# One layer with attention, retention and a squared-ReLU MLP: the sums of the first MLP product on one engine only, and one staging buffer at another address

## Chip, cores and metric

The kernel runs on one core of a Trainium2 chip. Its time is the device time of one execution in microseconds (us). A core has five engines that work at once, each through its own queue in program order: TensorE (PE in the profile; its weight loads are PEld), VectorE (DVE), ScalarE (ACT), GpSimd (POOL) and SyncE (SP), which here only issues the transfers between HBM and the on-chip memory.

## What is computed

The last stage of the layer is this MLP, in float32, on 2048 tokens of 1024 features:

```python
h = x * (1.0 + sc2) + sh2
f = jnp.square(jax.nn.relu(h @ w_ff1[l])) @ w_ff2[l]
x = layer_norm(ALPHA * x + gt2 * f, ln2_g[l], ln2_b[l])
```

w_ff1 is 1024 x 4096, w_ff2 is 4096 x 1024. Ahead of it stand the input norm, the conditioning, two mixers (latent attention and retention) and their output product; the change doesn't touch them.

## The kernel before, in words

**Precision.** Each float32 operand of a matmul is split in two: ScalarE rounds it to a high part (line 128), and an engine subtracts that to give a low part (line 131). A product is then three matmuls, high by high, low by high and high by low (lines 136 to 138, `mm3`).

**The first MLP product** (`split_h` and `up`) uses a Strassen-like scheme with seven block products P1 to P7 in place of eight. The tokens are taken in two halves; in each half sixteen steps c each make 256 of the 4096 columns, and the loop takes them in pairs (c, c+1) through the seven products in turn, so a pair is 14 products of 12 matmuls 128x512 each: P1, P1, P5, P5, P6, P6, P7, P7, P2, P2, P3, P3, P4, P4, on the accumulators u_X, u_Z, u_Y, u_W, and again u_X, u_Z, u_W. For each c four blocks of w1 (`w`, 128x512) are loaded into two buffers per block position; four of the seven products need a sum or a difference of blocks first, made in place (line 1077 in `prod`), before ScalarE and VectorE split the result into `w1h` and `w1l`. The ring of `w1h` and `w1l` holds five products (W1B).

**The choice of engine.** Line 1077 runs on VectorE where half is 0 and c is below 4 (W1V), and on GpSimd everywhere else: 16 times and 112 times. `split_h` makes the activation operands (`hh`, `hl`) of the seven products once per half, each in two pieces of 128x1024: a difference of blocks (line 1060) where the product needs one, and the split. For half 0 both pieces are on VectorE; for half 1, done during the last pair of half 0, the first piece is VectorE's and the second GpSimd's.

**Behind the products** VectorE adds accumulators (lines 1104 to 1122: `u`, `v`), ScalarE applies relu and square (lines 1093, 1094) and SyncE stores 256 KB to `g_d` (line 1095). `u` has two buffers, `v` three, and `r`, which takes the accumulator u_X directly, one. Spread over the same loop, a generator prepares w2 for the second product (`w2r`, `w2s`, lines 1132 to 1141) on VectorE and ScalarE.

**The second MLP product** (`down`) starts when the first ends. It loads `a` from `g_d` (line 1266) and its weights `wP` from `wt_d` (line 1276), splits `a` into `gP1h`, `gP1l` and so on, and accumulates in d_W, d_Z, d_X. Its pools lie where the pools of the first product lay, so a load into them waits until the earlier tile at that address is read or stored.

**What sets the order.** A scheduler with a timeline model of its own orders each engine's instructions when the kernel is built; each engine then works strictly in that order. The pools of the first product are stacked in the order of the tuple HSO: numbers are the operand pools of the seven products (index 0 to 6), "u" the pool of `u` and `v`, "w" that of `w1h` and `w1l`, "s" that of `w2s`, and "o" that of `r` (2 KB of each partition).

Of the kernel before, what the change touches and what calls it, by code (L numbers as in the profile page):

```python
# [14 lines left out]
OP = mybir.AluOpType  # L15
# [33 lines left out]
NLA = 3  # L49
HSS = "VVVVVVV"  # L50
HSL = "VVVVVVV"
HSO = 6, 5, "u", 4, 3, 2, "s", "o", 1, "w", 0
SRT = 29
LB = 18
HFB = 4
# [11 lines left out]
W1V = 4  # L67
# [50 lines left out]
def build(nc, tc, I, out, upto=9, dbg=None):  # L118
    dbg = {} if dbg is None else dbg
    V, A, G, T, Q = nc.vector, nc.scalar, nc.gpsimd, nc.tensor, nc.sync  # L120
# [3 lines left out]
    def split(x, hi, lo, hi_eng=None, lo_eng=None, log=None):  # L124
        hi_eng = hi_eng or A
        lo_eng = lo_eng or V
        if hi_eng is A:
            A.activation(hi, x, AF.Copy)  # L128
        else:
            hi_eng.tensor_copy(hi, x)  # L130
        i = lo_eng.tensor_tensor(lo, x, hi.bitcast(F32), op=OP.subtract)  # L131
        if log is not None:
            log.append(i.ins)

    def mm3(ps, sh, sl, mh, ml, start, stop, more=False):
        T.matmul(ps, sh, mh, start=start, stop=False, skip_group_check=more)  # L136
        T.matmul(ps, sh, ml, start=False, stop=False, skip_group_check=more)  # L137
        T.matmul(ps, sl, mh, start=False, stop=stop, skip_group_check=more)  # L138
# [805 lines left out]
    for n in range(2):  # L944
        p = (wo0, wo1)[n]
        wo.append([[p.tile([P, 512], R32, name=f"wo_{x}{n}_{k}") for x in "hl"] for k in range(KD)])
        for i in range(4):
            st = WOS[n][i]
            ks = range(2 * i, 2 * i + 2)
# [82 lines left out]
    hs4 = [None] * 7  # L1032
    for i in HSO:
        if i == "w":
# [10 lines left out]
    def split_h(half, o):  # L1045
        raw = {}
        for j, n in ((0, 0), (0, 1), (1, 1), (1, 0)):
            raw[j, n] = t = hraw.tile([P, 4, 512], F32, tag="raw", name=f"h4_{half}_{j}{n}")
            Q.dma_start(t, h2_d[border[2 * half + n]].rearrange("k p c -> p k c")[:, 4 * j:4 * j + 4, :])
        b11, b12, b22, b21 = raw[0, 0], raw[0, 1], raw[1, 1], raw[1, 0]  # L1050
        for x, (name, src, sub) in enumerate((("P1", b11, None), ("P5", b12, (b12, b11)), ("P6", b12, (b22, b12)),
                                              ("P7", b11, (b12, b11)), ("P2", b21, None), ("P3", b22, None),
                                              ("P4", b12, (b21, b12)))):
            p = hs4[x]
            hh = p.tile([P, 4, 512], R32, tag="hh", name=f"hh{half}_{name}")
            hl = p.tile([P, 4, 512], R32, tag="hl", name=f"hl{half}_{name}")
            for q in range(2):
                ks = slice(2 * q, 2 * q + 2)
                if sub:
                    (V, G if half else EN[HSS[x]])[q].tensor_tensor(src[:, ks], sub[0][:, ks], sub[1][:, ks], op=OP.subtract)  # L1060
                split(src[:, ks], hh[:, ks], hl[:, ks], A, (V, G if half else EN[HSL[x]])[q])
            o[name] = hh, hl
            yield

    def up(half, c, H):
        raw = []
        for m, j in ((0, 0), (1, 0), (1, 1), (0, 1)):
            t = w1r.tile([P, 512], F32, tag=f"r{m}{j}", name=f"w1_{half}_{c}_{m}{j}")
            with tc.issue_after(wodma) if half == 0 and c < 2 else nullcontext():
                Q.dma_start(t, I["w_ff1"][2 * c + m][:, 4 * j:4 * j + 4].rearrange("p k c -> p (k c)"))  # L1070
            raw.append(t)
        a11, a21, a22, a12 = raw
        ps = {}

        def prod(name, src, op, ch, start, sub=None):
            if sub:
                (V if half == 0 and c < W1V else G).tensor_tensor(src, *sub, op=op)  # L1077
            wh = w1p.tile([P, 512], R32, tag="wh", name=f"w1h{half}_{c}_{name}")
            wl = w1p.tile([P, 512], R32, tag="wl", name=f"w1l{half}_{c}_{name}")
            split(src, wh, wl, A, V, lows)  # L1080
            if start:
                ps[ch] = psf[c % 2].tile([P, 512], F32, tag="f", name=f"u{half}_{c}_{ch}")
            hh, hl = H[name]
            for k in range(4):
                ks = slice(k * P, (k + 1) * P)
                mm3(ps[ch], wh[:, ks], wl[:, ks], hh[:, k], hl[:, k], start and k == 0, k == 3, not start)

        def o(name, tag="o"):
            return (o4 if tag == "o" else o4b).tile([P, 512], F32, tag=tag, name=f"{name}{half}_{c}", bufs=dict(o=OO, u=2, v=OV)[tag])

        def act(x, m, n):
            r = o("r") if x is ps["X"] else x
            A.activation(r, x, AF.Relu)
            A.activation(r, r, AF.Square)
            Q.dma_start(g_d[2 * c + m][:, (2 * half + n) * 512:(2 * half + n + 1) * 512], r)

        prod("P1", a11, None, "X", True)
        yield
        prod("P5", a21, OP.add, "Z", True, (a21, a22))
        u = o("u", "u")  # L1100
        A.activation(u, ps["X"], AF.Copy)
        yield
        prod("P6", a21, OP.subtract, "Y", True, (a21, a11))
        V.tensor_tensor(u, u, ps["Y"], op=OP.add)
        yield
        prod("P7", a11, OP.subtract, "W", True, (a22, a21))
        v = o("v", "v")
        V.tensor_tensor(v, u, ps["Z"], op=OP.add)
        yield
        prod("P2", a12, None, "X", False)  # L1110
        V.tensor_tensor(v, v, ps["W"], op=OP.add)
        act(v, 1, 1)
        yield
        prod("P3", a21, OP.subtract, "Z", False, (a12, a21))
        act(ps["X"], 0, 0)
        yield
        prod("P4", a22, None, "W", False)
        v = o("v", "v")
        V.tensor_tensor(v, u, ps["Z"], op=OP.add)
        act(v, 0, 1)  # L1120
        v = o("v", "v")
        V.tensor_tensor(v, u, ps["W"], op=OP.add)
        act(v, 1, 0)
# [24 lines left out]
    NCH = DFF // 256  # L1148
    H = {}
    first = split_h(0, H)  # L1150
    for half in range(2):
        todo = work(range(8 * half, 8 * half + 8))
# [3 lines left out]
        count = 0  # L1156
        Hn = {}
        nxt = split_h(1, Hn) if half == 0 else None
        for c in range(0, NCH, 2):
            pair = [up(half, x, H) for x in (c, c + 1)]  # L1160
# [236 lines left out]
```

## Time and profile before

| what | us |
|---|---|
| median of three runs (2575.91 to 2579.59) | 2579.45 |
| the profiled execution, its own time | 2581.13 |
| its span, first to last instruction | 2579.4 |
| TensorE busy in the span | 2435.3 |
| VectorE busy | 1791.5 |
| ScalarE busy | 1218.5 |
| GpSimd busy | 1134.5 |

The first MLP product lies between 1276 and 1938 us of the span: its first matmul starts at 1276.2, half 1 begins at about 1626, and the last matmul starts at 1937.6. The second product follows to the end. In the timeline views a row gives start, duration, engine, line, operation, written and read tile, a count where equal neighbours are merged, and in brackets the idle time before it with what ended that. Durations of neighbours on an engine overlap a little, so the pace of a queue is read from start to start.

### The profile page before, as it was taken

The page shows a single profiled execution, that of the slowest core. Times are in us where ns is not written, and L with a number is a line of the kernel's source. Part 1 is how long each engine was busy: PE and PEld are TensorE (multiplying, and loading weights), DVE is VectorE, ACT ScalarE, POOL GpSimd, SP SyncE. Part 2 cuts the span into 40 slices and gives each one's busy share as a digit, 9 for nine tenths or more (in the row PEclk, how much of TensorE's full clock was granted, in tenths as well). Part 3 has the DMA queues.
Part 4 walks back from the last instruction along what each step waited for, and adds up shares of the span by engine and source line. Part 5 has one row for each costly group of instructions (what it writes and reads, how often), then busy time and mean ns, then how long its engine had stood idle before and what let it go on. Part 6 is the DMA issues. An engine that isn't in the chain of part 4 may idle for free.

```text
span 2579.4 us, 34040 instructions
## 1 busy us (share of the span) xinstructions
PE 2435.3 (94%) x11668; PEld 2019.9 (78%) x11668; DVE 1791.5 (69%) x2904; ACT 1218.5 (47%) x2380; POOL 1134.5 (44%) x1078
## 2 busy tenths in 40 slices
PE   5999999999999999899989999999998999999997
PEld 5887778877878888778768877788877888878886
DVE  8757576556767676754668878777874666786676
ACT  4653222246777777634455555555643211232114
POOL 4322554647979897643202335523322211372122
PEclk9999999989999999999989999999998999999998
DMA  9457342011111110446467766577667777677773
GB/s 332 152 188 243 99 128 69 33 46 59 36 49 38 46 48 28 150 154 219 147 216 276 244 233 208 190 268 253 230 228 281 277 268 271 257 280 272 272 273 145
DMA packets 205341, 464.71 MB, mean 180 GB/s; under 512 B 18792, under 2 KB 52968, under 8 KB 190832
## 3 DMA queue, kind: packets, MB, share of 16 engines
q1 hardware_dynamic: 205168, 462.54, 51.5%
q8 instruction: 92, 1.51, 0.2%
q14 instruction: 81, 0.66, 0.1%
HBM read 313.30 MB, written 149.17 MB: 179 GB/s over the span
## 4 chain that ended last, share of the span: by engine, by line
PE 55%; DVE 17%; DMA 12%; ACT 7%; issue 6%; POOL 3%; SPq 0%; DVEq 0%; ACTq 0%; POOLq 0%
PE d_W L138 4%; PE d_W L136 4%; PE d_W L137 4%; PE t L839 3%; DMA wt_d<-w2s 3%; DVE w1l_P L131 2%; DMA wad<-in_w_ada 2%; DMA g_d<-r 2%; PE pj L138 2%; PE o L832 2%; PE pj L136 2%; PE pj L137 2%; PE o L830 2%; PE d_Z L136 2%; PE d_Z L137 2%
## 5 line engine op out<-in xcount | busy, mean ns | idle before, releaser
L1077 POOL TENSOR_TENSOR w<-w,w 128x512 f32<-128x512 f32 x112 | 183.0, 1642 | 380.2 <-DMA w<-in_w_ff 296.3
L131 DVE TENSOR_TENSOR w1l_P<-w,w1h_P 128x512 fp32r<-128x512 f32 x224 | 200.8, 901 | 78.3 <-ACT w1h_P L128 75.1
L811 ACT ACTIVATE p<-s,nm 128x512 f32<-128x512 f32 (+3 forms) x320 | 196.8, 628 | 41.1 <-DVE nm L808 37.5
L1221 POOL TENSOR_TENSOR zt<-zt,ag 128x512 f32<-128x512 f32 x32 | 53.8, 1699 | 362.9 <-DMA zt<-z_d 266.4
L806 DVE TENSOR_REDUCE mx<-s 128x1 f32<-128x512 f32 (+3 forms) x288 | 175.2, 620 | 54.2 <-PE s L138 51.4
L855 POOL TENSOR_TENSOR tl<-tf,th 128x512 fp32r<-128x512 f32 x144 | 184.9, 1296 | 1.7
L839 PE MATMUL t<-ident,p 128*128 128x128 f32 x1088 | 165.5, 278 | 4.8 <-ACT tf L850 1.7
L839 PEld LDWEIGHTS t<-ident,p 128*128 128x128 f32 x1088 | 131.3, 143 | 29.3 <-ACT tf L850 5.8
L136 PE MATMUL pj<-wbh,hhb 128*128 128x512 f32 x384 | 150.9, 395 | 1.2 <-ACT wbh L128 0.8
L137 PE MATMUL pj<-wbl,hhb 128*128 128x512 f32 x384 | 151.3, 394 | 0.2 <-DVE wbl L131 0.2
L138 PE MATMUL pj<-wbh,hlb 128*128 128x512 f32 x384 | 151.4, 395 | 0.0
L128 ACT ACTIVATE w1h_P<-w 128x512 fp32r<-128x512 f32 x224 | 135.2, 618 | 25.6 <-PE u_Y L137 7.6
L136 PE MATMUL s<-kt,qt 96*128 96x512 f32 (+3 forms) x320 | 129.4, 405 | 12.7 <-ACT p L811 10.2
L128 ACT ACTIVATE w2s<-w2r 128x512 fp32r<-128x512 f32 x112 | 70.2, 630 | 133.5 <-DVE w2r L1138 64.7
L832 PE MATMUL o<-tl,v 128*128 128x512 f32 (+2 forms) x320 | 124.5, 398 | 4.9 <-DVE tl L131 4.7
L830 PE MATMUL o<-th,v 128*128 128x512 f32 (+2 forms) x320 | 123.1, 389 | 6.1 <-DVE osum L866 5.3
L137 PE MATMUL s<-kt,qt 96*128 96x512 f32 (+3 forms) x320 | 119.9, 375 | 3.7 <-DVE kt L131 3.7
L131 DVE TENSOR_TENSOR w2s<-w2r,w2s 128x512 fp32r<-128x512 f32 x112 | 95.0, 851 | 38.4 <-ACT w2s L128 37.9
L138 PE MATMUL s<-kt,qt 96*128 96x512 f32 (+3 forms) x320 | 119.5, 374 | 0.0
L131 DVE TENSOR_TENSOR tl<-t,th 128x512 fp32r<-128x512 f32 (+3 forms) x176 | 92.3, 538 | 25.3 <-ACT th L128 24.2
L136 PE MATMUL u_Z<-hh_P,w1h_P 128*128 128x512 f32 x256 | 102.1, 399 | 7.4 <-DVE z L1000 3.7
L138 PE MATMUL u_W<-hh_P,w1l_P 128*128 128x512 f32 x256 | 100.8, 394 | 7.9 <-DVE w1l_P L131 7.9
(383 smaller groups left out, 7694.2 us busy)
## 6 DMA issues: line engine op xcount, KB each, us to landing
wP<-wt_d SPq DMA_DIRECT2D x112, 1024.0 KB, 5.4
wt_d<-w2s SPq DMA_DIRECT2D x112, 512.0 KB, 3.6
w<-in_w_ff SPq DMA_DIRECT2D x128, 256.0 KB, 4.3
a<-g_d SPq DMA_DIRECT2D x32, 1024.0 KB, 11.6
g_d<-v SPq DMA_DIRECT2D x96, 256.0 KB, 3.6
wad<-in_w_ada SPq DMA_DIRECT2D x64, 256.0 KB, 2.9
w2r<-in_w_ff SPq DMA_DIRECT2D x16, 1024.0 KB, 8.7
x<-in_x SPq DMA_DIRECT2D x16, 512.0 KB, 8.3
```

The source lines that it names most:

```text
L128: A.activation(hi, x, AF.Copy)
L131: i = lo_eng.tensor_tensor(lo, x, hi.bitcast(F32), op=OP.subtract)
L136: T.matmul(ps, sh, mh, start=start, stop=False, skip_group_check=more)
L137: T.matmul(ps, sh, ml, start=False, stop=False, skip_group_check=more)
L138: T.matmul(ps, sl, mh, start=False, stop=stop, skip_group_check=more)
L806: V.tensor_reduce(mx[:, j:j + 1], ps[:, :n], op=OP.max, axis=AX.X)
L811: A.activation(pt[:, :m], b[:, :m], AF.Exp, bias=nm, accum_out=rs[:, qi, j:j + 1])
L830: T.matmul(po[:, cs], w, th[:, cs], start=(done == 0), stop=False)
L832: T.matmul(po[:, cs], w, tl[:, cs], start=False, stop=(done == nk))
L839: T.transpose(tp[:, qi * P:(qi + 1) * P], pts[h, 4 * qb + qi, kb // 4][1][:, kb % 4 * P:(kb % 4 + 1) * P], ident)
L855: (V if mode == "C" else G).tensor_tensor(tl[:, cs], tf[:, cs], th[:, cs].bitcast(F32), op=OP.subtract)
L1077: (V if half == 0 and c < W1V else G).tensor_tensor(src, *sub, op=op)
```

## The change

It does two things. All sums and differences of line 1077 and all pieces of the activation operands (line 1060, and line 131 where it writes `hl`) go to VectorE, whatever the half and c; GpSimd has no instruction left in the first MLP product. And the pool "o" of `r` is stacked right behind that of `u` and `v`, so the five pools that lay between move up by 2 KB and `r` lies at another address.

```diff
-HSO = 6, 5, "u", 4, 3, 2, "s", "o", 1, "w", 0
+HSO = 6, 5, "u", "o", 4, 3, 2, "s", 1, "w", 0
...
                 if sub:
-                    (V, G if half else EN[HSS[x]])[q].tensor_tensor(src[:, ks], sub[0][:, ks], sub[1][:, ks], op=OP.subtract)
-                split(src[:, ks], hh[:, ks], hl[:, ks], A, (V, G if half else EN[HSL[x]])[q])
+                    V.tensor_tensor(src[:, ks], sub[0][:, ks], sub[1][:, ks], op=OP.subtract)
+                split(src[:, ks], hh[:, ks], hl[:, ks], A, V)
...
             if sub:
-                (V if half == 0 and c < W1V else G).tensor_tensor(src, *sub, op=op)
+                V.tensor_tensor(src, *sub, op=op)
```

The scheduler also orders the queues anew. Nothing moves on any engine ahead of step c = 4 of half 0. Three places follow, each as the difference of one engine's order: rows with a minus stand so before, rows with a plus after.

VectorE, at the end of the pair c = 10, 11 of half 0, where the first difference for half 1 waits for its load (`h_1_01` is a block of activations, `w1l_11_P` the low part of that pair's last product, `w_0_12_10` a block of w1 of the next pair):

```order
 L1132 TENSOR_TENSOR w2r_16819<-w2r_16819,gt_14750 128x1024
-L1060 TENSOR_TENSOR h_1_01_17283<-h_1_01_17283,h_1_00_17281 128x1024
 L131 TENSOR_TENSOR w1l_11_P_16850<-w_0_11_11_16566,w1h_11_P_16849 128x512
 L131 TENSOR_TENSOR w2s_0_16875<-w2r_16819,w2s_0_16875 128x512
+L1060 TENSOR_TENSOR h_1_01_17283<-h_1_01_17283,h_1_00_17281 128x1024 x2
+L1077 TENSOR_TENSOR w_0_12_10_16881<-w_0_12_10_16881,w_0_12_11_16883 128x512
 L131 TENSOR_TENSOR w1l_12_P_16888<-w_0_12_00_16879,w1h_12_P_16887 128x512
```

The low part of the last product moves ahead of the difference that waits, and both pieces of that difference and a sum of the next pair stand in the queue behind it.

VectorE, in the last pair of half 0 (c = 14, 15), where the activation operands of half 1 are made:

```order
 L131 TENSOR_TENSOR w1l_14_P_17405<-w_0_14_00_17227,w1h_14_P_17404 128x512
-L131 TENSOR_TENSOR hl_P_17290<-h_1_00_17281,hh_P_17289 128x1024
+L131 TENSOR_TENSOR hl_P_17290<-h_1_00_17281,hh_P_17289 128x1024 x2
 L131 TENSOR_TENSOR w1l_15_P_17425<-w_0_15_00_17256,w1h_15_P_17424 128x512
 L131 TENSOR_TENSOR w1l_14_P_17452<-w_0_14_01_17233,w1h_14_P_17451 128x512
-L131 TENSOR_TENSOR hl_P_17345<-h_1_01_17283,hh_P_17344 128x1024
+L131 TENSOR_TENSOR hl_P_17345<-h_1_01_17283,hh_P_17344 128x1024 x2
 L1104 TENSOR_TENSOR u_14_17313<-u_14_17313,u_14_Y 128x512
 L1060 TENSOR_TENSOR h_1_01_17283<-h_1_11_17285,h_1_01_17283 128x1024
 L131 TENSOR_TENSOR w1l_15_P_17472<-w_0_15_01_17262,w1h_15_P_17471 128x512
+L1060 TENSOR_TENSOR h_1_01_17283<-h_1_11_17285,h_1_01_17283 128x1024
```

Each piece that was GpSimd's now stands in VectorE's queue beside its twin; the row of the fourth product of step 14, the first one shown, is where the count of the prediction begins.

SyncE, from the first product's last stores to the second product's first weights:

```order
+L1276 DMA wP_0_0_20401<-wt_d_0_64 128x2048
 L1095 DMA g_d<-v_14_20153 128x512
-L1095 DMA g_d<-v_15_20173 128x512
-L1095 DMA g_d<-r_14_20232 128x512
-L1095 DMA g_d<-r_15_20253 128x512
-L1276 DMA wP_0_0_20401<-wt_d_0_64 128x2048
 L1276 DMA wP_0_1_20435<-wt_d_0_64 128x2048
-L1095 DMA g_d<-v_14_20273 128x512
 L1276 DMA wP_0_0_20473<-wt_d_1_65 128x2048
 L1276 DMA wP_0_1_20508<-wt_d_1_65 128x2048
+L1095 DMA g_d<-v_15_20173 128x512
```

And ScalarE at the same place (`gP1h` is the first operand of the second product):

```order
-L1093 ACTIVATE r_15_20253<-u_15_X 128x512
-L1094 ACTIVATE r_15_20253<-r_15_20253 128x512
 L1093 ACTIVATE v_14_20273<-v_14_20273 128x512
 L1094 ACTIVATE v_14_20273<-v_14_20273 128x512
 L1093 ACTIVATE v_14_20278<-v_14_20278 128x512
+L1094 ACTIVATE v_14_20278<-v_14_20278 128x512
 L1093 ACTIVATE v_15_20299<-v_15_20299 128x512
-L1094 ACTIVATE v_14_20278<-v_14_20278 128x512
-L1094 ACTIVATE v_15_20299<-v_15_20299 128x512
 L128 ACTIVATE gP1h_0_0_20403<-a_0_0_00_20393 128x1024
```

The first weight load moves ahead of four stores, `r` of step 15 among them; the second weight load, which waited for the store of `r` of step 15, now waits for no store; and that `r` itself moves behind the operands of the second product. On VectorE the first three low parts of the second product (`gP1l` twice, `gP5l`) move ahead of the last add of the first product (the last of line 1122).

## Rows read from the trace of the kernel before

**Rows 1.** Windows: stretch, length, busy us (instructions) of each engine, granted clock, DMA.

```profile
1525.00:1660.00 135.00, 122.50 (x513) 97.09 (x512) 111.97 (x112) 75.99 (x128) 72.47 (x36) 0.97 0.63 209
1660.00:1895.00 235.00, 234.00 (x1026) 191.89 (x1025) 184.10 (x242) 137.49 (x245) 78.76 (x49) 1.00 0.71 241
1938.00:1958.00 20.00, 12.92 (x37) 9.77 (x37) 10.24 (x10) 7.36 (x10) 1.02 (x1) 0.66 0.98 371
```

**Rows 2.** Timeline of TensorE in an undisturbed stretch; 48 matmuls from start to start.

```profile
1704.40 0.39 PE L136 MATMUL u_X<-hh_P,w1h_P 128*128 128x512 f32 x1
...
1715.28 0.39 PE L136 MATMUL u_Y<-hh_P,w1h_P 128*128 128x512 f32 x1
```

**Rows 3.** Groups of VectorE, 1300 to 1370 us, GpSimd idle: busy us, mean ns.

```profile
L131 DVE TENSOR_TENSOR w1l_P<-w,w1h_P 128x512 fp32r<-128x512 f32 x20 | 13.6, 687 | 9.6 <-ACT w1h_P L128 9.5
L131 DVE TENSOR_TENSOR hl_P<-h,hh_P 128x1024 fp32r<-128x1024 f32 x6 | 7.1, 1219 | 6.1 <-ACT hh_P L128 6.1
L1077 DVE TENSOR_TENSOR w<-w,w 128x512 f32<-128x512 f32 x8 | 5.5, 688 | 0.7 <-DMA w<-in_w_ff 0.6
```

**Rows 4.** Groups of VectorE, 1525 to 1660 us, GpSimd working.

```profile
L131 DVE TENSOR_TENSOR w1l_P<-w,w1h_P 128x512 fp32r<-128x512 f32 x44 | 51.7, 1181 | 12.1 <-ACT w1h_P L128 10.8 <-DMA w<-in_w_ff 1.0
L131 DVE TENSOR_TENSOR hl_P<-h,hh_P 128x1024 fp32r<-128x1024 f32 x7 | 17.2, 2457 | 0.3 <-ACT hh_P L128 0.3
L131 DVE TENSOR_TENSOR w2s<-w2r,w2s 128x512 fp32r<-128x512 f32 x14 | 12.3, 882 | 6.8 <-ACT w2s L128 6.8
L1138 DVE TENSOR_TENSOR w2r<-w2r 128x512 f32<-128x512 f32 x8 | 7.7, 958 | 0.0
```

**Rows 5.** Groups of GpSimd, 1525 to 1660 us.

```profile
L1077 POOL TENSOR_TENSOR w<-w,w 128x512 f32<-128x512 f32 x25 | 41.3, 1661 | 52.9 <-DMA w<-in_w_ff 36.5 <-DVE w1l_P L131 13.2 <-issue 1.4
L131 POOL TENSOR_TENSOR hl_P<-h,hh_P 128x1024 fp32r<-128x1024 f32 x7 | 20.8, 2968 | 5.2 <-ACT hh_P L128 5.2
L1060 POOL TENSOR_TENSOR h<-h,h 128x1024 f32<-128x1024 f32 x4 | 11.5, 2864 | 19.3 <-DMA w<-in_w_ff 19.0
```

**Rows 6.** Timeline of VectorE in the last pair of half 0.

```profile
1581.59 1.79 DVE L1138 TENSOR_TENSOR w2r<-w2r 128x512 f32<-128x512 f32 x1
...
1586.72 1.78 DVE L131 TENSOR_TENSOR w2s<-w2r,w2s 128x512 fp32r<-128x512 f32 x1
...
1589.03 0.68 DVE L131 TENSOR_TENSOR w2s<-w2r,w2s 128x512 fp32r<-128x512 f32 x1
1589.63 1.78 DVE L131 TENSOR_TENSOR w1l_P<-w,w1h_P 128x512 fp32r<-128x512 f32 x1
1591.33 3.43 DVE L131 TENSOR_TENSOR hl_P<-h,hh_P 128x1024 fp32r<-128x1024 f32 x1
```

**Rows 7.** Timeline of TensorE: first stall after 1525 us; first use of a low part.

```profile
1533.09 0.50 PE L138 MATMUL u_W<-hh_P,w1l_P 128*128 128x512 f32 x1 [2.40 <-DVE w1l_P L131]
...
1592.05 0.39 PE L138 MATMUL u_W<-hh_P,w1l_P 128*128 128x512 f32 x1
```

**Rows 8.** Timeline of TensorE at the passage to the second product.

```profile
1937.64 0.39 PE L138 MATMUL u_W<-hh_P,w1l_P 128*128 128x512 f32 x1
1942.36 0.76 PE L136 MATMUL d_W<-wP,gP1h 128*128 128x512 f32 x1 [4.34 <-DMA wP<-wt_d]
...
1948.86 2.08 PE L138 MATMUL d_W<-wP,gP1l 128*128 128x512 f32 x4 [2.74 <-DVE gP1l L131]
```

**Rows 9.** Timeline of ScalarE at the passage.

```profile
1934.73 0.60 ACT L1093 ACTIVATE r<-u_X 128x512 f32<-128x512 f32 x1 [2.50 <-DMA g_d<-r]
...
1939.16 1.98 ACT L128 ACTIVATE gP1h<-a 128x1024 fp32r<-128x1024 f32 x2
```

**Rows 10.** Timeline of VectorE at the passage.

```profile
1946.98 0.69 DVE L1122 TENSOR_TENSOR v<-u,u_W 128x512 f32<-128x512 f32 x1 [10.35 <-DMA g_d<-v]
```

**Rows 11.** Timeline of SyncE's queue at the passage.

```profile
1936.43 3.49 SPq L1276 DMA_DIRECT2D wP<-wt_d  x2
```

**Rows 12.** Tile w (blocks of w1), 1300 to 1930 us: its loads.

```profile
DMA to landing us min/median/max: 2.6/4.2/8.9
```

## The prediction

> **What bounds the kernel now.** I read the windows of the stage first. TensorE's pace comes from an undisturbed stretch: 48 matmuls in 10.88 us [rows 2], 0.2267 us each. A window's length less its matmuls at that pace is what TensorE lost there. From 1525 to 1660 us that is 135 - 513 x 0.2267 = 18.7 us, from 1660 to 1895 us 235 - 1026 x 0.2267 = 2.4 us, and from 1938 to 1958 us, the passage to the second MLP product, 20 - 37 x 0.2267 = 11.6 us [rows 1]. So in most of the first product TensorE is the bound and a saving elsewhere is worth nothing; there are 32.7 us to win, in two places.
>
> Then I asked who is waited for. In the first place TensorE waits for the low part of w1 from VectorE, 2.40 us the first time [rows 7]. VectorE is slow there, not only busy: `w1l` takes 1181 ns and `hl` 2457 ns while GpSimd works, against 687 and 1219 ns where GpSimd is idle [rows 3, 4]. In the timeline one such operation follows the last after 0.60 us alone, and after 1.70 us beside GpSimd [rows 6]. In the passage, TensorE waits 4.34 us for the first weights and 2.74 us for a low part [rows 8].
>
> **Part 1, GpSimd's work to VectorE, 1525 to 1660 us.** The work added to VectorE is 25 sums, 7 `hl` and 4 differences [rows 5], at VectorE's own price [rows 3]: 25 x 0.688 + 7 x 1.219 + 4 x 1.219 = 30.6 us. What it gets back, with GpSimd gone, is the stretch of its own operations [rows 4]: 44 `w1l` from 51.7 to 30.2, 7 `hl` from 17.2 to 8.5, 14 `w2s` from 12.3 to 9.6, 8 of line 1138 from 7.7 to 5.5, in all 35.1 us. VectorE's 112.0 us [rows 1] become 107.5. The load is about even; what changes is when the work comes due.
>
> The tight piece is the last pair of half 0. From the fourth product's low part of step 14 (the last but one in [rows 6]) to that of the second P5 product of half 1, the new order has 14 `hl` and 8 differences, 1.14 us apart (my estimate: 1.219 less the overlap that takes 0.68 to 0.60), and 23 operations 0.60 us apart: 38.9 us. TensorE does 11 products of 12 matmuls in that time, 29.9 us. VectorE falls back by 9.0 us, and how much of it TensorE feels depends on its lead. Before, the lead at that point was some 0.7 us: the operation ends at 1591.33, where the next one starts [rows 6], and the first matmul that takes its result starts at 1592.05 [rows 7]. In the ten microseconds ahead, four operations were stretched by 1.1 us each, three of which stand in [rows 6]; these 4.4 us come back, and six sums of 0.60 take 3.6. The lead becomes 1.5. I add 1.25 us for `r`, whose single buffer makes ScalarE wait for a store (2.50 us in [rows 9]; half, as VectorE has a queue to work off meanwhile). The clock adds some: a mean of 0.97 over 135 us [rows 1] means about 8 us at the lower of the two levels, 1.2 GHz, so 4 us lost; I keep half. What is left is 9.0 - 1.5 + 1.25 + 2.0 = 10.75 us, and the gain 18.7 - 10.75 = 8.0 us. The first stall of this stretch, 2.40 us [rows 7], is in it: there `w1l` no longer stands behind a difference that waits for its load. Ends: no lead won, the whole wait for `r` and the whole loss by the clock leave 9.0 - 0.7 + 2.5 + 4.0 = 14.8 us, a gain of 3.9; a full ring of five products would cover everything, 18.7.
>
> **Part 2, the 49 sums from 1660 to 1895 us.** They cost VectorE 49 x 0.688 = 33.7 us on top of 184.1 in 235 [rows 1], even if nothing came back, and TensorE has 2.4 us to win. I take 1.5, between 0 and 2.4. The sums of steps 4 to 11 of half 0 lie where TensorE loses nothing: 0, hidden by its matmuls. If that cover went, the price is that of the third rival.
>
> **Part 3, the buffer of `r` and the passage.** Before, the first weights are issued at 1936.43 [rows 11], behind the store of step 15's `r`, which ScalarE can compute only at 1934.73, after 2.50 us of waiting for the store before it [rows 9]. In the new order the weights are issued ahead of those stores and none waits for `r`'s address. They should have landed before TensorE's last matmul of the product at 1937.64. Next late is `gP1h`: it starts at 1939.16 now [rows 9], behind 1.2 us of operations on that `r` which move behind it, so about 1937.9; its first half is there 1.0 us later, at 1939. TensorE then idles about 1.1 us instead of 4.5. The second stall came from VectorE, which stood 10.35 us before an add whose buffer was still being stored [rows 10], with `gP1l` queued behind; now `gP1l` stands ahead. It is ready at 1940.2, before the eight matmuls that need only high parts have ended. With 1.5 us for the clock, whose mean was 0.66 in this window [rows 1], 2.6 us stay lost: a gain of 9.0. Ends: 11.6, all of it; and 2.0, if the stores that ScalarE's last operations need are themselves held up behind five weight loads of 1 MB, the transfer engines being 0.98 busy in that window already [rows 1], so that `gP1h` is late all the same.
>
> **Sum.** 8.0 + 1.5 + 9.0 = 18.5 us off the profiled execution's 2581.1: 2562.6. That execution stands 1.7 us above the median of the runs, so the time predicted is **2561**. All upper ends together give 32.7 us, 2546.7; all lower ends 5.9 us, 2573.5.
>
> **Rivals.** *VectorE cannot carry it.* By its busy time VectorE would need 112.0 + 30.6 = 142.6 us in a stretch of 135 [rows 1, 5], if the stretched operations kept their length. It would become the bound there, 7.6 us later than now; with the passage 9.0 earlier the time is 2578, no change. Against it stand 687 and 1181 ns for one operation [rows 3, 4]; I give it 0.07. The Trainium skill, Perfetto Trace Analysis, holds occupancy to be a fair measure of how near VectorE is to its limit (section Identifying the Most-Contended Engine), and that offloading a saturated VectorE, to GpSimd even, may make sense (section Optimizing Scalar/DVE Operations); by that rule taking work off GpSimd would be wrong here, and the time this rival's. The same paragraph doubts such an offload between these two because they share a port, and on this the trace agrees: 1181 against 687 ns.
>
> *The move of `r` does nothing*, because something else holds the first operand or the weights: only parts 1 and 2 count, 9.5 us, 2570. For it speaks that ScalarE's last `v` operations stay ahead of `gP1h`; against it, the weights are the last to come in the first stall [rows 8]. 0.10.
>
> *Loads stop VectorE's queue.* GpSimd could wait for blocks of w1 without harm; of its idle time in [rows 5], 36.5 us were such waits. In VectorE's queue the first sum of each step waits for a load that is issued only after the same buffer's last read, four operations earlier, and every low part behind it waits too. A load lands after 4.2 us [rows 12], four operations take 2.4, so a pair loses 2 x 1.8 = 3.6 us. A pair takes TensorE 168 x 0.2267 = 38.1 us, and I count 30.5 us of VectorE's work in it (14 low parts, 8 sums, 10 adds and 11.3 us on w2), so 7.6 are free. It decides from a landing of 6.2 us; the longest is 8.9 [rows 12]. At 7.0, each of 14 pairs loses 2 x 4.6 - 7.6 = 1.6 us, 22 in all, parts 1 and 2 give nothing, and with the passage it is 13 us slower: about 2593. For it: the range of landings; against it, in [rows 3] eight sums on VectorE waited 0.6 us for loads in all. 0.06.
>
> **How the numbers follow.** The forecast has 0.77. The range of 2547 to 2573 is that of its ends and takes in the second rival; the first and third lie outside, with a little of the forecast's own tail. This kernel's measurement can tell about 0.2%, 5.2 us, from no change. Faster by more: forecast and second rival, 0.87. Within: the first rival, 0.07. Slower: the third, 0.06.
>
> **What would show it.** No GpSimd work from about 1370 us to the end of the product; `w1l` near 690 ns and `hl` near 1220 throughout; the matmuls of 1525 to 1660 us done some 8 us sooner, with what stall remains at the start of half 1; at the passage one idle time of TensorE near 1 us, with `gP1h` and not the weights ending it, and none for `gP1l`. It is wrong if VectorE's rows of line 1077 show long waits for loads, if `w1l` stays above 800 ns, or if the first d_W matmul still waits for `wP`.

## The result and the profile after

The changed kernel takes 2551.98 us (median of 4 runs, 2542.38 to 2555.32), against 2579.32 for the kernel before (4 runs): a ratio of 0.9891, interval 0.9872 to 0.9910. 27.3 us came off; forecast were 18.5. The profiled execution took 2555.32, so 25.8 less than that of before.

The windows of the changed kernel, same columns as [rows 1], the last one the 20 us from the end of the first product:

```profile
1525.00:1660.00 135.00, 133.70 (x588) 110.03 (x588) 118.18 (x171) 89.10 (x150) 0.00 (x0) 1.00 0.67 231
1660.00:1895.00 235.00, 235.00 (x1038) 194.58 (x1038) 186.73 (x291) 140.39 (x247) 0.00 (x0) 1.00 0.77 257
...
1918.00:1938.00 20.00, 15.81 (x63) 12.76 (x63) 16.30 (x14) 11.51 (x16) 4.65 (x3) 0.91 0.98 339
```

And one stretch of the kernel before that [rows 1] leave out, from 1895 us to the last matmul of the product:

```profile
1895.00:1938.00 43.00, 41.32 (x180) 33.26 (x178) 26.38 (x34) 22.22 (x40) 11.00 (x7) 1.00 0.64 216
```

A window's length less its matmuls at 0.2267 us [rows 2] is again what TensorE lost; matmuls that straddle an edge make this good to about 0.5 us.

| stretch | lost before | forecast | lost after |
|---|---|---|---|
| 1525 to 1660, around the start of half 1 | 18.7 | 10.7 | 1.7 |
| 1660 to 1895 | 2.4 | 0.9 | 0 |
| 1895 to the end of the product | 2.2 | not looked at | 0 |
| 20 us from there, the passage | 11.6 | 2.6 | 5.7 |

The gains are 17.0, 2.4, 2.2 and 5.9, in all 27.5 us. The profiled execution shows 25.8: its first product began 4.1 us later (first matmul at 1280.34 against 1276.20 us) and lost 1.6 us less up to 1345 us, both ahead of the first difference in any queue; the rest are the windows' edges. Over all profiled executions of this study that start lies between 1269 and 1280 us, though no queue is in another order ahead of it. So some 10 us of scatter come from stages that the change doesn't touch, and what is worth a few us is read below from the windows, not from the times.

VectorE's groups from 1525 to 1660 us, which answer to [rows 3, 4]:

```profile
L131 DVE TENSOR_TENSOR w1l_P<-w,w1h_P 128x512 fp32r<-128x512 f32 x50 | 34.1, 690 | 6.3 <-ACT w1h_P L128 6.0
L1077 DVE TENSOR_TENSOR w<-w,w 128x512 f32<-128x512 f32 x32 | 21.6, 688 | 2.6 <-DMA w<-in_w_ff 2.5
L131 DVE TENSOR_TENSOR hl_P<-h,hh_P 128x1024 fp32r<-128x1024 f32 x14 | 16.7, 1230 | 0.0
```

These VectorE operations have their undisturbed length: 690 ns in place of 1181, 1230 in place of 2457. The 32 sums waited 2.5 us for loads, and no wait of TensorE follows from that.

What is left of stalls from 1345 us to the passage, in TensorE's timeline:

```profile
1618.19 0.50 PE L136 MATMUL u_Z<-hh_P,w1h_P 128*128 128x512 f32 x1 [0.72 <-ACT w1h_P L128]
1621.82 0.50 PE L138 MATMUL u_Z<-hh_P,w1l_P 128*128 128x512 f32 x1 [0.58 <-DVE w1l_P L131]
1922.35 0.50 PE L136 MATMUL d_W<-wP,gP1h 128*128 128x512 f32 x1 [4.19 <-ACT gP1h L128]
```

The passage in the other queues. SyncE:

```profile
1901.87 0.33 SPq L1276 DMA_DIRECT2D wP<-wt_d  x1
1906.56 0.33 SPq L1095 DMA_DIRECT2D g_d<-v  x1
1906.98 1.35 SPq L1276 DMA_DIRECT2D wP<-wt_d  x3
1908.44 0.58 SPq L1095 DMA_DIRECT2D g_d<-v  x1
1909.06 0.54 SPq L1276 DMA_DIRECT2D wP<-wt_d  x1
```

VectorE:

```profile
1920.00 0.69 DVE L1119 TENSOR_TENSOR v<-u,u_Z 128x512 f32<-128x512 f32 x1 [3.83 <-DMA g_d<-v]
```

ScalarE:

```profile
1920.72 0.63 ACT L1093 ACTIVATE v<-v 128x512 f32<-128x512 f32 x1 [3.22 <-DVE v L1119]
1921.25 1.99 ACT L128 ACTIVATE gP1h<-a 128x1024 fp32r<-128x1024 f32 x2
```

The weights are early now, issued at 1901.87, 16 us ahead of the product's end. But five loads of 1 MB stand among the stores of `v`, four of them ahead of the store issued at 1908.44; that store frees its buffer only at 1920, the add of line 1119 waits for it, ScalarE's relu waits for the add, and `gP1h` stands behind the relu in ScalarE's queue.

### The profile page after: what moved, and what is told of

The parts are those of the page before. It is cut to its first block, busy times and chain, and to the rows that moved or that the text cites. A ratio compares the mean times of both kernels' runs of the same rounds, so it can differ in the third digit from the quotient of the medians.

```text
span 2553.5 us, 33901 instructions
## 1 busy us (share of the span) xinstructions
PE 2420.6 (95%) x11668; PEld 2014.6 (79%) x11668; DVE 1785.5 (70%) x3027; ACT 1221.4 (48%) x2380; POOL 919.1 (36%) x955
## 4 chain that ended last, share of the span: by engine, by line
PE 60%; DVE 14%; DMA 11%; ACT 6%; issue 5%; POOL 4%; SPq 0%; DVEq 0%; ACTq 0%; POOLq 0%
PE d_W L136 4%; PE d_W L138 4%; PE d_W L137 4%; PE t L839 3%; DMA wad<-in_w_ada 2%; PE pj L138 2%; PE pj L137 2%; PE pj L136 2%; PE o L830 2%; PE o L832 2%; PE d_Z L137 2%; PE d_Z L136 2%; PE d_Z L138 2%; PE s L136 2%; PE s L138 2%
## 5 line engine op out<-in xcount | busy, mean ns | idle before, releaser
L131 DVE TENSOR_TENSOR w1l_P<-w,w1h_P 128x512 fp32r<-128x512 f32 x224 | 153.6, 689 | 41.6 <-ACT w1h_P L128 41.1
L1077 DVE TENSOR_TENSOR w<-w,w 128x512 f32<-128x512 f32 x128 | 86.9, 689 | 30.4 <-DMA w<-in_w_ff 25.9
L136 PE MATMUL psY<-wo_h,mh 128*128 128x512 f32 x256 | 101.5, 398 | 3.8 <-ACT wo_h L128 2.2
## 6 DMA issues: line engine op xcount, KB each, us to landing
a<-g_d SPq DMA_DIRECT2D x32, 1024.0 KB, 11.6
```

Of the source, the lines that this page charges most:

```text
L1077: V.tensor_tensor(src, *sub, op=op)
```

## The experiments

The theory: work of GpSimd on the on-chip memory stretches VectorE's operations, and that made the stalls of the first product; at the passage a store behind weight loads is late. The rivals: the stalls came from waiting for what GpSimd delivered; the address of `r` did it; VectorE is near its limit.

### One part at a time

`r` alone, on the kernel before:

```diff
-HSO = 6, 5, "u", 4, 3, 2, "s", "o", 1, "w", 0
+HSO = 6, 5, "u", "o", 4, 3, 2, "s", 1, "w", 0
```

> Only the address of r is changed; sums and pieces stay on GpSimd as before. Theory (contention on VectorE made the stalls of the first product, the address of r only the passage): TensorE loses the same 18.7 us in the last pairs of half 0 and the start of half 1, some 4.6 us over the rest of half 1, and less than the 11.6 us at the passage, 2 to 6, since the first weights no longer wait for r's store and no store of v stands ahead of the first operand in the new order; 2570 to 2574 us. Rival (the passage was helped by the engine change): the passage keeps 11 us or more, 2579 us.

Measured: 2570.51 us, ratio 0.9977 (0.9967 to 0.9987). The stretch around half 1's start lost 18.5 us, as before, the passage 7.5 in place of 11.6:

```profile
1525.00:1660.00 135.00, 122.94 (x514) 98.62 (x513) 112.94 (x113) 78.40 (x133) 71.91 (x35) 0.96 0.63 211
...
1940.00:1960.00 20.00, 14.85 (x55) 11.70 (x55) 10.37 (x9) 8.01 (x13) 3.59 (x2) 0.83 1.03 356
```

```profile
1950.86 0.69 DVE L1119 TENSOR_TENSOR v<-u,u_Z 128x512 f32<-128x512 f32 x1 [9.28 <-DMA g_d<-v]
```

The passage lost more than the 2 to 6 us expected. The weights no longer come last, but VectorE waited 9.28 us for a store of `v`, with the second `gP1l` behind that add, and TensorE 4.82 us for it. So the first product's gain isn't from `r`, and at the passage another wait took over.

The engines alone, on the changed kernel with the old tuple HSO:

> All sums and pieces on VectorE, r at its old address. Theory: the stretch before and after the half boundary loses 1 to 3 us in place of 18.7, the rest of half 1 under 1 in place of 4.6, and the passage keeps 11 to 12 us with the weights as the last to come; 2556 to 2559 us. Rival (the engine change also helps the passage): the passage loses 6 us, 2552 us.

Measured: 2549.13 us, ratio 0.9900 (0.9883 to 0.9917).

```profile
1525.00:1660.00 135.00, 135.00 (x596) 111.55 (x595) 117.32 (x170) 88.43 (x148) 0.00 (x0) 1.00 0.67 233
...
1914.50:1934.50 20.00, 14.86 (x53) 11.72 (x54) 13.83 (x11) 9.12 (x13) 2.27 (x2) 0.83 1.01 392
```

Nothing is lost around half 1's start, and 8.0 us at the passage: the expected 11 to 12 didn't come, nor the rival's 6. Even with `r` at its old address the weights were not last; TensorE waited 1.31 us for `gP1h` and 3.83 for `gP1l`, whose queue stood 6.78 us before an add that waited for a store of `v`. The whole change is no faster than this part of it: 0.9891 and 0.9900 with intervals that overlap. The address of `r` is worth 4 us on the kernel before. On top of the engine change the two traces differ by 2.3 us in its favour at the passage and by 1.8 against it at half 1's start.

Sums on VectorE, the second pieces of half 1 on GpSimd as before:

```diff
-                    V.tensor_tensor(src[:, ks], sub[0][:, ks], sub[1][:, ks], op=OP.subtract)
-                split(src[:, ks], hh[:, ks], hl[:, ks], A, V)
+                    (V, G if half else EN[HSS[x]])[q].tensor_tensor(src[:, ks], sub[0][:, ks], sub[1][:, ks], op=OP.subtract)
+                split(src[:, ks], hh[:, ks], hl[:, ks], A, (V, G if half else EN[HSL[x]])[q])
```

> Sums of w1 blocks on VectorE, second pieces of half 1's activation operands on GpSimd as before, r at the new address. Theory (GpSimd's work stretches VectorE's): some 32 us of GpSimd work in the last pair still stretch VectorE there, so 4 to 9 us are lost at the boundary, with the low part of w1 named at the stalls; none in the rest of half 1; about 2557 us. Rival (GpSimd's own pieces, 2.97 us each, come too late for TensorE): the stalls at the boundary name hl, nearly all 18 us stay, about 2569 us.

Measured: 2555.22 us, 0.9920 (0.9902 to 0.9939); 13.3 us lost around half 1's start, more than expected, nothing in the rest of half 1.

```profile
1525.00:1660.00 135.00, 124.90 (x537) 101.08 (x536) 117.85 (x147) 81.56 (x138) 34.30 (x11) 0.99 0.60 207
```

VectorE's groups in that stretch:

```profile
L131 DVE TENSOR_TENSOR hl_P<-h,hh_P 128x1024 fp32r<-128x1024 f32 x7 | 12.9, 1846 | 0.0
...
L1060 DVE TENSOR_TENSOR h<-h,h 128x1024 f32<-128x1024 f32 x3 | 9.0, 3010 | 0.0
```

Five of the six stalls there name `w1l`, one an add of `v`, none `hl`: TensorE waited for VectorE, not for GpSimd's pieces. ScalarE did wait 3.94 us for one of GpSimd's differences, but VectorE's queue has no gap behind that. Eleven operations on GpSimd were enough for most of the old loss.

The pieces on VectorE, the 112 sums on GpSimd as before:

```diff
-                V.tensor_tensor(src, *sub, op=op)
+                (V if half == 0 and c < W1V else G).tensor_tensor(src, *sub, op=op)
```

> All pieces of the activation operands on VectorE, 112 sums of w1 blocks on GpSimd as before, r at the new address. Theory: each sum on GpSimd still stretches about one VectorE operation by 1.1 us, and VectorE has more to do at the boundary: 8 to 14 us lost there and the 4.6 us of the rest of half 1 stay; w1l near 900 ns; about 2565 us. Rival (only the pieces on GpSimd were late): the boundary loses 1 to 3 us, 2552 to 2556 us.

Measured: 2560.27 us, 0.9938 (0.9917 to 0.9960); 9.4 us lost from 1525 to 1660 us, `w1l` at 888 ns there.

```profile
1525.00:1660.00 135.00, 128.30 (x554) 104.16 (x553) 119.77 (x135) 85.10 (x141) 51.05 (x31) 0.99 0.63 215
```

So both halves of the engine change count, and the pieces more than their number says, since they fall where VectorE has no slack. Two of this run's five stalls aren't contention alone: the longest, 2.53 us at 1529.37, follows a VectorE difference that waited 3.51 us for its load, and one of 1.79 us at 1611.72 follows ScalarE's wait of 1.58 us for a sum from GpSimd. The rest of half 1 lost less than expected, 0.1 us up to 1895.

### GpSimd work that nobody waits for

The first try added idle work after each low part of w1 and after each piece (128x256, two or four or eight at a time, into a scratch tile):

> The changed kernel, and beside it idle work on GpSimd: two 128x256 operations on each low part of w1 whose sum was GpSimd's before, and four or eight of them on each piece that was GpSimd's, all read finished operands and write a scratch tile that nobody reads. Theory (GpSimd beside VectorE stretches VectorE's operations): w1l rises from 689 ns to 850 to 950, the half boundary loses 10 to 25 us and half 1 some 3 to 15, with w1l named at TensorE's stalls; 2565 to 2590 us. Rival (the stalls came from waiting for what GpSimd had to deliver): nobody waits for this work, so w1l stays near 690 ns and the time near 2552 us.

Measured: 2603.22 us, 1.0111 (1.0094 to 1.0128), beyond the expected range. It isn't clean. VectorE's group of `w1l` from 1345 to 1900 us:

```profile
L131 DVE TENSOR_TENSOR w1l_P<-w,w1h_P 128x512 fp32r<-128x512 f32 x183 | 140.1, 769 | 35.8 <-POOL scr L1090 19.7 <-ACT w1h_P L128 12.8 <-issue 3.0
```

VectorE waited 19.7 us for GpSimd, since the idle work read ring buffers that `w1l` is written to. The stretch to 769 ns is there, but waiting is mixed in. The next three hang on one operand that stays until the end of half 1; the orders of TensorE, VectorE and ScalarE are the changed kernel's, and nobody waits for GpSimd. In `split_h`, behind the split of the first product's second piece (60 two-input operations here; 100 of one input in the second kernel):

```diff
+                if half and q and name == "P1":
+                    G.tensor_tensor(scr, hl[:, 2, 0:256].bitcast(F32), hl[:, 3, 0:256].bitcast(F32), op=OP.subtract)
+                    for i in range(60):
+                        G.tensor_tensor(scr, scr, scr, op=OP.subtract)
```

> The changed kernel, and 61 two-input 128x256 operations on GpSimd that begin when the low part of half 1's first activation operand is there and run one after another on a scratch tile; no other engine waits for any of them, and the orders of the other engines are the changed kernel's. At about 1 us each they last some 60 us over the half boundary. Theory (contention alone makes VectorE slow): VectorE's operations with two on-chip operands are stretched there by half or more, the boundary loses 8 to 25 us in place of 1.9 with w1l named at the stalls, nothing elsewhere; 2560 to 2577 us. Rival (what hurt in the kernel before, and in the first run with idle work, was waiting for GpSimd's results or buffers): 1.9 us at the boundary, 2552 us.

> The same with 100 one-input operations (times a constant, plus a constant) of 128x256 in place of the 60 two-input ones. If any work of GpSimd on the on-chip memory slows VectorE: the boundary loses 5 us or more here too, 2557 us or more. If it needs GpSimd's two-input form: 1.9 us stay and the time is near 2552 us. If waiting was the cause all along, both kernels stay near 2552 us.

Measured: 2553.42 us with two inputs and 2548.46 with one, losses of 3.7 and 4.9 us from 1525 to 1660 us against 1.7:

```profile
1525.00:1660.00 135.00, 132.14 (x579) 108.11 (x578) 123.57 (x163) 84.84 (x142) 72.50 (x54) 1.00 0.63 214
```

```profile
1525.00:1660.00 135.00, 130.82 (x574) 107.01 (x573) 122.30 (x165) 85.94 (x144) 70.56 (x90) 1.00 0.63 217
```

The first expectation failed. In the second kernel the loss is near the 5 us of its first case, but the time isn't near 2557 us: a loss this small lies within the scatter of the other stages. VectorE in the two-input kernel (its line 1084 is 1077 elsewhere):

```profile
1609.29 2.35 DVE L131 TENSOR_TENSOR hl_P<-h,hh_P 128x1024 fp32r<-128x1024 f32 x2
...
1613.36 0.68 DVE L131 TENSOR_TENSOR w1l_P<-w,w1h_P 128x512 fp32r<-128x512 f32 x1
...
1617.95 4.16 DVE L1084 TENSOR_TENSOR w<-w,w 128x512 f32<-128x512 f32 x4
```

GpSimd in the same kernel, 1590 to 1615 us, then 1618 to 1628:

```profile
L1068 POOL TENSOR_TENSOR scr<-scr 128x256 f32<-128x256 f32 x9 | 28.7, 3193 | 0.7
L1068 POOL TENSOR_TENSOR scr<-scr 128x256 f32<-128x256 f32 x11 | 10.4, 942 | 0.9
```

Up to 1617 VectorE is undisturbed and GpSimd stands back, 3193 ns for one small operation; behind that the two alternate and VectorE's operations follow each other after 1.02 us in place of 0.60. One input on GpSimd costs VectorE 0.1 to 0.2 us per operation. Contention is there in both, with the price on either side. Operations of the size that the kernel before had were still to be tried (30 of 128x512, with a bf16 result):

```diff
+                if half and q and name == "P1":
+                    for i in range(30):
+                        G.tensor_tensor(scr, hl[:, 2].bitcast(F32), hl[:, 3].bitcast(F32), op=OP.subtract)
```

> The changed kernel, and 30 two-input operations of 128x512 on GpSimd (the size of the sums it had; the result is written as bf16 into a scratch tile) that begin when the low part of half 1's first activation operand is there and run one after another; nobody waits for them and the other engines' orders are the changed kernel's. Theory (contention, and its price goes with the size of GpSimd's operation: 0.42 us with 128x256 in the run before, 1.1 with 128x512 in the kernel before): VectorE's operations beside them are stretched to some 1.7 us, the boundary loses 7 to 20 us in place of 1.9, with w1l at the stalls; 2558 to 2570 us. Rival (VectorE in a dense row of on-chip operations shuts GpSimd out, whatever the size, and the kernel before lost its time by waiting for GpSimd): GpSimd's operations last 3 us and more while VectorE keeps 0.60, the boundary loses under 5, 2555 us or less.

Measured: 2576.67 us (10 runs), 0.9996 (0.9981 to 1.0011). Thirty operations that nobody needs take back the whole gain: 27.8 us lost from 1525 to 1660 us, more than expected.

```profile
1525.00:1660.00 135.00, 117.08 (x473) 92.03 (x473) 124.17 (x140) 72.15 (x119) 59.92 (x30) 0.92 0.57 193
```

VectorE beside them (line 1063 is 1060 elsewhere, 1117 is 1111):

```profile
1609.35 4.55 DVE L131 TENSOR_TENSOR hl_P<-h,hh_P 128x1024 fp32r<-128x1024 f32 x2
1613.83 1.75 DVE L131 TENSOR_TENSOR w1l_P<-w,w1h_P 128x512 fp32r<-128x512 f32 x1
1615.50 2.28 DVE L1063 TENSOR_TENSOR h<-h,h 128x1024 f32<-128x1024 f32 x1
1617.70 0.67 DVE L1117 TENSOR_TENSOR v<-v,u_W 128x512 f32<-128x512 f32 x1
```

One operation follows the last 1.67 us after a `w1l`, near the 1.70 beside GpSimd in [rows 6], and 2.2 us after a piece. The add of line 1117, which takes one operand from an accumulator, keeps 0.60. So contention alone, without any wait for GpSimd, makes a loss of this size. TensorE's stalls here name adds of VectorE and `w1h` more than `w1l`, which the expectation had; `w1h` waits in turn for VectorE's sums.

In the kernel before not all of the 18.7 us was contention. Its first stall, 2.40 us at 1533.09 [rows 7], followed these two operations of VectorE:

```profile
1529.05 1.23 DVE L1060 TENSOR_TENSOR h<-h,h 128x1024 f32<-128x1024 f32 x1 [3.42 <-DMA h<-h_d]
1530.19 2.84 DVE L131 TENSOR_TENSOR w1l_P<-w,w1h_P 128x512 fp32r<-128x512 f32 x1
```

The difference waited for its load and the low part behind it was stretched; the new order takes this low part out from behind the difference. And the last stall of that stretch, 1.50 us at 1636.39, came behind a wait of 3.16 us of ScalarE for the store of `r`.

### How near VectorE is to its limit

The same idle work as in the first try (its part on w1), on VectorE:

```diff
+            if sub and not (half == 0 and c < W1V):
+                for i in (0, 256):
+                    V.tensor_tensor(scr, wl[:, i:i + 256].bitcast(F32), wl[:, i:i + 256].bitcast(F32), op=op)
```

> The changed kernel with the same idle work put on VectorE: two 128x256 operations for each of the 112 sums that moved, which by half of the 0.60 us of a 128x512 one and something over are 0.3 to 0.4 us each, 67 to 90 us in all. Theory (in each pair 30.5 us of VectorE's work stand against 38.1 us of TensorE's, so the sums are covered with room left): 36 us per pair still fit, TensorE loses nothing in the steady part, 2 to 8 us at the half boundary; 2552 to 2560 us. Rival (VectorE is at its limit and each added us is paid): 30 us or more are lost in half 1, 2580 us or more.

Measured: 2554.48 us, 0.9919 (0.9904 to 0.9934); 421 ns each.

```profile
1525.00:1660.00 135.00, 129.70 (x559) 105.61 (x558) 131.41 (x221) 86.55 (x146) 0.00 (x0) 0.97 0.62 215
1660.00:1895.00 235.00, 235.00 (x1038) 194.60 (x1037) 221.36 (x398) 139.46 (x248) 0.00 (x0) 1.00 0.74 257
```

In half 1 VectorE does 34.6 us more (221.36 against 186.73), is busy 94%, and TensorE loses nothing. Around half 1's start 13.2 us more cost 6.6. VectorE is the bound at that place, where its timeline in the changed kernel shows no gap from 1573.71 to 1630.78 us, and not in the rest of half 1.

### The passage

On the changed kernel, the third to fifth weight load behind the store of step 14's third `v` (a list keeps the stores):

```diff
-            wdma.append(Q.dma_start(w.bitcast(F32), wt_d[s][x][q]).ins)
+            with tc.issue_after(stores[-4]) if 2 <= len(wdma) < 5 else nullcontext(): wdma.append(Q.dma_start(w.bitcast(F32), wt_d[s][x][q]).ins)
```

> The changed kernel with the third to fifth weight load of the second product queued behind the store of step 14's third v. Theory (what is late at the passage is VectorE's add into a v buffer whose store stands behind those loads, and gP1h behind it): the add no longer waits 3.8 us, gP1h starts by 1916 of the changed kernel's time, TensorE's 4.2 us wait falls under 0.8 and the passage's loss from 6.1 to 0.5 to 2.5 us; 2547 to 2549 us. Rival (ScalarE's own queue or the load of a is what is late, or the weights come late now): TensorE still waits 2 us or more, named after wP or gP1h, 2552 us.

The same with the old tuple HSO and `1 <= len(wdma) < 5`:

> All of the first product's sums and pieces on VectorE, r at its old address, and the second to fifth weight load queued behind the store of step 14's third v. Theory (same cause): the add that waited 6.8 us for a store waits under 2, gP1l is there in time, and the passage loses 1 to 3.5 us in place of 8.3, the half boundary stays at 0.2; 2543 to 2546 us, the shortest of all. Rival (the old address of r keeps the weights late): TensorE waits 3 us or more for wP, 2549 us.

Measured: 2544.21 us, 0.9883 (0.9868 to 0.9898), and 2546.30, 0.9889 (0.9874 to 0.9904). The passages lose 1.2 and 2.8 us, against 5.7 and 8.0 without the queueing:

```profile
1915.80:1935.80 20.00, 18.69 (x83) 15.41 (x83) 16.52 (x14) 10.72 (x14) 2.15 (x2) 1.00 0.98 381
```

```profile
1911.80:1931.80 20.00, 17.48 (x76) 14.07 (x76) 15.84 (x13) 10.30 (x14) 2.70 (x2) 1.00 1.02 407
```

In the first the same add of line 1119 has no wait, and `gP1h` follows 0.6 us after the last matmul of the product (1915.51), against 3.5 us in the changed kernel:

```profile
1913.82 0.68 DVE L1119 TENSOR_TENSOR v<-u,u_Z 128x512 f32<-128x512 f32 x1
...
1916.12 1.99 ACT L128 ACTIVATE gP1h<-a 128x1024 fp32r<-128x1024 f32 x2
```

That shows the cause at the passage, although the scheduler also put other operations there in a new order, and TensorE still waits 1.31 us for `gP1h` where under 0.8 was expected. In the second the add that had waited 6.78 us waits 4.14, not under 2 as expected, and TensorE waits 1.21 us for `gP1l`:

```profile
1914.68 0.69 DVE L1122 TENSOR_TENSOR v<-u,u_W 128x512 f32<-128x512 f32 x1 [4.14 <-DMA g_d<-v]
```

Both have the lowest medians of the study; against the changed kernel the gain is in the windows, 4.5 us in the first, while the intervals of the ratios overlap.

## Why the prediction was right, and where its sizes were off

**The direction and its reason held.** The forecast had VectorE's load come out even (107.5 for 112.0 us); it is 118.18 with 15% more matmuls done in the window. The rival that VectorE cannot carry it falls with the run that loads VectorE more still. The rule of the Trainium skill, Perfetto Trace Analysis, that stood beside that rival takes occupancy as the measure: here 94% in half 1 cost nothing, while before 83% beside GpSimd (112.0 of 135 us, [rows 1]) went with 18.7 us lost. The rival on loads falls too: the sums waited 2.5 us for loads from 1525 to 1660 us.

**Part 1 was mis-sized: 8.0 forecast, 17.0 measured.** All four terms of 9.0 - 1.5 + 1.25 + 2.0 = 10.75 us were off the same way. The lead of 1.5 was the worst. These rows of the changed kernel, VectorE then TensorE, answer to [rows 6, 7]:

```profile
1585.14 2.36 DVE L131 TENSOR_TENSOR hl_P<-h,hh_P 128x1024 fp32r<-128x1024 f32 x2
```

```profile
1590.12 0.39 PE L138 MATMUL u_W<-hh_P,w1l_P 128*128 128x512 f32 x1
```

The low part is done at 1585.14 and used at 1590.12: a lead of 5.0. I credited the stretch of ten microseconds alone. Read in the same way for each product, the lead at the last pair's start was 4.4 us before and 6.2 after, and at the pair's second product 1.4 and 4.8. From there to the seventh it fell by 0.7 before and rose by 0.2 after, about the 0.8 that I credited; the other 3.4 us VectorE had won further ahead. With the engines alone changed the lead at this point was 6.7, and nothing was lost. Next, the work was counted too high: six differences stand in that stretch of the queue, not eight, so it took 36.5 us (1585.14 to 1621.68) in place of 38.9, and VectorE fell back by 6.6. The wait for `r` came to 0.43 us on ScalarE and cost nothing, and the clock stayed at full speed (1.00). 6.6 - 5.0 = 1.6 us, and 1.7 were lost.

**Part 2**: 2.4 for 1.5, inside its ends. The stretch from 1895 us on, where the kernel before lost 2.2 us in the same way, was left out of the sum.

**Part 3 was too high: 9.0 forecast, 5.9 measured**, and the step that failed is that `gP1h` would start 1.2 us earlier, freed of `r`. The lower end named what happened, stores that ScalarE needs held up behind five weight loads; it cost 3.1 us of the 9.0. The move of `gP1l` ahead of the last add did what was said: no wait for it is left. That `r`'s address kept the weights late was true of the kernel before, but the engine change alone ended that as well; the credit to `r` was too large.

In the windows the sum was 27.5 for 18.5 us, as far off as part 1 by itself: that part 3 came out 3.1 lower, and part 2 and the stretch left out 0.9 and 2.2 higher, cancelled by chance. The time fell inside the range because its upper end had part 1's 18.7, which was nearly reached.

## What to carry to other kernels

Work that is handed to GpSimd to relieve VectorE is paid on VectorE where VectorE's operations read two on-chip operands: count what it stretches there before what it takes off, above all where VectorE has little lead. Read the lead (when a result is ready against when it is used) over a whole pair of steps on both sides of a tight place, not over the last few operations. Early weight loads can make a late store: when a pool has few buffers, look for the stores that stand behind the loads.

## What the runs showed of the hardware

The price on VectorE goes with the size of GpSimd's operation. What an operation is delayed is the start-to-start time less that without GpSimd: 0.42 us beside 128x256 (1.02 less 0.60), 1.1 beside 128x512 (1.70 less 0.60, [rows 6]), 2.2 beside 128x1024 (1591.33 to 1594.68 in the trace of before, 3.35 less 1.14). Beside 128x256 with one input it is 0.20 at most (0.80 less 0.60). GpSimd's own times, shortest, median and longest in ns, are these, in the kernels with two and one inputs and then in the kernel before:

```profile
L1068 POOL TENSOR_TENSOR scr<-scr x60: 613/942/6869, 1587.4 to 1666.5; 128x256 f32<-128x256 f32 x60
```

```profile
L1068 POOL TENSOR_SCALAR scr<-scr x100: 407/720/3049, 1586.2 to 1666.7; 128x256 f32<-128x256 f32 x100
```

```profile
L1077 POOL TENSOR_TENSOR w<-w,w x112: 1280/1680/2282, 1370.7 to 1911.8; 128x512 f32<-128x512 f32 x112
...
L131 POOL TENSOR_TENSOR hl_P<-h,hh_P x7: 2413/2859/3376, 1590.8 to 1643.2; 128x1024 fp32r<-128x1024 f32 x7
```

In all four the delay is GpSimd's shortest time less some 0.2 us, so it grows by whole operations and isn't a share. The medians, taken beside VectorE's work, are longer. Adds with one operand in an accumulator weren't stretched, 0.67 to 0.70 us in every run. The Trainium skill, SBUF — State Buffer (SBUF: two separate sides), has this as an exclusive lock, held for a whole instruction, where VectorE has two on-chip inputs and GpSimd's operation reads on-chip memory; the delays here agree but for those 0.2 us.

Who stands back isn't fixed: in dense rows of its own VectorE kept small operations of GpSimd waiting 3 us each for 27 us, and operations of 128x512 not. No run shows what decides it; this stays open.
